# A hybrid decoder trunk: roots and decay exponents moved to GpSimd, the inverse's scratch moved to the residual's tiles, and a priority for each kind of mixer work

## The chip, the core and the metric

One core of a Trainium2 chip runs the whole program. The time is the device time of one execution in microseconds (us). The core's engines are named as in the profile: PE (TensorE, matrix multiplies; PEld is its weight load), DVE (VectorE), ACT (ScalarE), POOL (GpSimd) and SP (SyncE, which here issues most DMAs). PSUM is the memory that PE writes its results to; SBUF holds everything else on the core.

## The reference

Two layers over 256 tokens of 1,024 features in float32. Each layer is a half-step SwiGLU feed-forward, a token mixer, and another half-step feed-forward, each between two RMS norms:

```python
f = swiglu_ffn(rmsnorm(x, pre), w_in, w_out)          # D_FF = 2816
x = x + 0.5 * rmsnorm(f, post)
p = rmsnorm(x, pre) @ mix_w_in                        # q k v z beta a | glu | two gates
y = (sig(g_a) * gated_deltanet(...) + sig(g_b) * conformer_conv(...)) @ mix_w_out
x = x + rmsnorm(y, post)
...                                                   # the second feed-forward
```

The mixer's first branch is a gated delta rule with 8 heads of 128 and chunks of 64 tokens. q, k and v pass a causal convolution of 4 taps and SiLU; q and k are normalized per head and token. With G the running sum of the log decay in a chunk:

```python
decay = where(causal, exp(where(causal, G[c] - G[s], 0)), 0)
a_mat = where(strict, (k @ k.T) * decay * beta, 0)
u, w  = solve(I + a_mat, [v * beta, k * beta * exp(G)])
qk    = (q @ k.T) * decay
v_new = u - w @ state                                  # chunk after chunk
o     = (q * exp(G)) @ state + qk @ v_new
state = state * exp(G[-1]) + k_dec.T @ v_new
out   = (rmsnorm(o, norm_w) * silu(z)) @ w_o
```

The other branch is a gated linear unit, a causal depthwise convolution of 31 taps, a layer norm, SiLU and a projection.

## The kernel before, in words

**Weights.** All weight matrices stream in pieces of 128 x 1,024 numbers (some 128 x 544), 222 per layer, 90 of them in the mixer. SP loads a piece into `raw` (3 buffers), ACT rounds it to `whi`, and DVE or POOL subtracts to give the rest `wlo` (L147 and L148, rings of 8). PE multiplies in three products (`mm3`, L391 to L393; `piece_ch`, L416 to L418, gives results with channels on partitions): whi by the rounded activations, wlo by them, and whi by their rest. The set `POOL` lists which of a mixer's 90 pieces have their `wlo` made on POOL; all others are DVE's.

**The mixer's order.** PE's order is written out by hand: PE runs in program order, and the program runs the projection's column chunks in the order of `PLAN` (g0, k1, g1, ka, kb, ...), where an entry's list names the jobs that start when its chunk ends. A job is a generator; `Lanes.tick`, called after every few matmuls of a chunk, lets each job take its next step once the number of ticks in `DELAY` has passed and the jobs in `AFTER` are done. A chunk also starts only when the jobs in `BEFORE` are finished. So the jobs' PE instructions stand between the chunks' matmuls. On DVE, ACT and POOL a scheduler orders the instructions by priority; `CFG` holds offsets for some kinds (`stat`, `conv`, `ev`, `post`, ...), and a block inside `prio(tc, key)` gets the offset of its key.

**The steps that matter here.** `decays` (L668 to L693) makes the running sums G with three small PE products, sends them through DRAM to have them along the free axis (`gx`), and makes 16 exponents min(gx - G, mask) on DVE (`dt`, L687), the mask being copied into the unused part of the sums' PSUM tile (L678); ACT then takes the exponential. `k_tokens` (`kt0`, `kt1`) transposes k (L700), sums squares per head, takes their inverse root with `rsqrt`, and scales. `similarities` (`sim0`, `sim1`) multiplies k by k (L744), times decay and beta, into `at` (L747). `inverse` (L771, L773) inverts 32 x 32 blocks in 62 DVE steps per layer on two scratch tiles, `ia` and `iu`; they are slots 16 and 17, which q's convolution output `qT` uses too, and `AFTER` has both `f_q0` and `f_q1` wait for `inv`. `merge` joins the blocks' inverses to those of 64 x 64 (L804 to L831). `q_tokens` (`qt0`, `qt1`) transposes q, and makes the products `qk` (L867, L870). `s0` and `s1` (L895 to L928) run the two chunk steps. `cn` is the layer norm of the other branch, `on0` and `on` the norm of o.

**Roots.** `rms_scale` (L265) takes an inverse root of one column with a power on POOL. All other inverse roots use `rsqrt`: a bit-shift seed and three Newton steps on DVE, 8 or 16 columns wide, in a PSUM tile as scratch (tag `tr`, three buffers, which the transposes, the similarities and the sums also use).

Of the kernel before, what the change touches and what calls it, by code (L numbers as in the profile page):

```python
# [15 lines left out]
P = 128  # L16
# [50 lines left out]
POOL = {2, 3, 5, 9, *range(15, 54), *range(55, 65), 67, 68, 88}  # L67

CFG = dict(stat=0, conv=-800, ev=300, tok=4, st=4, post=50, pre=100, fin=None, tokens=0)


class Lanes:


    def __init__(self):
        self.now, self.jobs, self.done = 0, [], set()
# [37 lines left out]
def prio(tc, key):  # L114
    return nullcontext() if CFG[key] is None else tc.high_priority(offset=CFG[key])


class Stream:
# [14 lines left out]
    def load_one(self, parts=1):  # L133
        nc, src = self.nc, self.pieces[self.nload]
        n = src.shape[-1]
        raw = self.pool.tile([P, D], F32, name="raw", tag="raw", bufs=3)
        hi = self.pool.tile([P, D], F32R, name="whi", tag="whi", bufs=RING)
        lo = self.pool.tile([P, D], F32R, name="wlo", tag="wlo", bufs=RING)
        nc.sync.dma_start(raw[:, :n], src)
        eng = nc.gpsimd if self.side[self.nload] else nc.vector  # L140
        self.loaded.append((hi, lo))
        self.nload += 1
        for i in range(parts):
            if i:
                yield
            c = slice(i * n // parts, (i + 1) * n // parts)
            nc.scalar.copy(hi[:, c], raw[:, c])  # L147
            eng.tensor_tensor(lo[:, c], raw[:, c], hi.bitcast(F32)[:, c], op=ALU.subtract)  # L148
# [11 lines left out]
def trunk(ctx: ExitStack, tc: tile.TileContext, x_in, wfirst, consts, feat, pch, tokp,  # L160
# [29 lines left out]
    def ps_gd(shape=None):  # L190
        return psum.tile(shape or [P, 4, P], F32, name="gd", tag="tr", bufs=3)
# [3 lines left out]
    V, S, T = nc.vector, nc.scalar, nc.tensor  # L195
# [15 lines left out]
    mhalf = cpool.tile([P, 1], F32, name="mhalf")  # L211
    V.memset(mhalf, -0.5)
# [11 lines left out]
    negmask = cst[:, K_MASK:K_MASK + P]  # L224
# [15 lines left out]
    def rsqrt(o, v, n, scratch=None):  # L240

        y = work.tile([P, n], F32, name="nw_y", tag=f"nw_y{n}", bufs=2)
        seed = y if scratch is None else scratch[:, n:2 * n]
        V.tensor_scalar(seed.bitcast(I32), v.bitcast(I32), 1, None, op0=ALU.logical_shift_right)
        V.tensor_scalar(y.bitcast(I32), seed.bitcast(I32), -1, 0x5F3759DF, op0=ALU.mult, op1=ALU.add)
        if n == 1:
            hv = work.tile([P, n], F32, name="nw_h", tag=f"nw_h{n}", bufs=2)
            a = work.tile([P, n], F32, name="nw_a", tag=f"nw_a{n}", bufs=2)
            V.tensor_scalar(hv, v, -0.5, None, op0=ALU.mult)
            for it in range(3):  # L250
                V.tensor_scalar(a, y, y, hv, op0=ALU.mult, op1=ALU.mult)
                V.tensor_scalar(o if it == 2 else y, a, 1.5, y, op0=ALU.add, op1=ALU.mult)
            return
        hv, a = scratch[:, 0:n], scratch[:, n:2 * n]
        V.tensor_scalar(hv, v, -0.5, None, op0=ALU.mult)
        for it in range(3):
            V.tensor_tensor(a, y, hv, op=ALU.mult)
            V.tensor_tensor(a, y, a, op=ALU.mult)
            V.scalar_tensor_tensor(o if it == 2 else y, a, 1.5, y, op0=ALU.add, op1=ALU.mult)

    def rms_scale(o, ms, more=None):

        V.tensor_scalar(ms, ms, RMS_EPS if more is None else more, None if more is None else RMS_EPS,  # L263
                        op0=ALU.add, **({} if more is None else dict(op1=ALU.add)))
        nc.gpsimd.tensor_tensor(o, ms, mhalf, op=ALU.pow)  # L265
# [6 lines left out]
    lanes = Lanes()  # L272
# [259 lines left out]
    def mixer(xt, l, after_mix):  # L532
# [88 lines left out]
        rq = small(16, "rq", bufs=1)  # L621
        ex = small(32, "ex", bufs=1)
# [6 lines left out]
        def decays():  # L629
# [44 lines left out]
            V.tensor_tensor(xin[:, 16:32], xin[:, 16:32], ps[:, 0:16], op=ALU.subtract)  # L674
            gr = stt("gr", [P, P])[0:16]
            S.copy(gr, ps[0:16, 128:256])
            mask = ps[:, 256:384]
            S.copy(mask, negmask)  # L678
            gd = dram.tile([16, P], F32, name=f"gd{l}")
            nc.sync.dma_start(gd, gr)  # L680
            for gp in range(2):
                gx = slot(6 + gp, [P, 8, P], name="gx")
                row = gd[gp * 8:gp * 8 + 8, :].rearrange("a b -> (a b)").rearrange("(o n) -> o n", o=1)
                nc.sync.dma_start(gx.rearrange("p a b -> p (a b)"), row.broadcast_to([P, D]))
                dt = slot(8 + gp, [P, 8, P], name="dt")
                for th in range(8):
                    V.scalar_tensor_tensor(dt[:, th, :], gx[:, th, :], G[:, gp * 8 + th:gp * 8 + th + 1], mask,  # L687
                                           op0=ALU.subtract, op1=ALU.min)
                S.activation(dt, dt, AF.Exp)
                if gp == 0:  # L690
                    S.activation(ex, xin, AF.Exp)
# [14 lines left out]
        def k_tokens(gp):  # L706
# [18 lines left out]
            V.tensor_tensor(kds[:, c], ex[:, 16 + gp * 8:24 + gp * 8], t8, op=ALU.mult)
# [8 lines left out]
        def similarity(gp):  # L734
# [140 lines left out]
        def q_scale():  # L875
            yield from ()
            rsqrt(rq, vq, 16, ps_gd([P, 512]))
# [144 lines left out]
        def conv_norm():  # L1022
            xh = []
            for tb in range(2):
# [15 lines left out]
                rsqrt(r, ve, 1)  # L1040
# [27 lines left out]
        def o_scale(tb):  # L1068
# [5 lines left out]
            rqt = rq.rearrange("p (g b h) -> p g b h", g=2, b=2)[:, :, tb, :]  # L1074
            v8 = small(8, "vo")
            ve = v8.rearrange("p (g h) -> p g h", g=2)
            pw = ps_gd([P, 512])
            sq8 = pw[:, 16:24].rearrange("p (g h) -> p g h", g=2)
            V.tensor_copy(sq8, rqt)
            V.tensor_tensor(sq8, rqt, sq8, op=ALU.mult)  # L1080
            V.tensor_tensor(ve, sso, sq8, op=ALU.mult)
            V.tensor_scalar(v8, v8, 1.0 / P, RMS_EPS, op0=ALU.mult, op1=ALU.add)
            r8 = small(8, "ro")
            ry = pw[:, 24:32]
            rsqrt(ry, v8, 8, pw[:, 0:16])
            ro = r8.rearrange("p (g h) -> p g h", g=2)
            V.tensor_tensor(ro, rqt, ry.rearrange("p (g h) -> p g h", g=2), op=ALU.mult)
# [180 lines left out]
```

## Time and profile before

| | |
|---|---|
| runs | 1409.2, 1406.61, 1408.67 us; median 1408.67 |
| profiled execution | 1408.11 us, of which the span is 1406.0 |
| busy | PE 1362.3 us (97%), DVE 945.5, ACT 748.8, POOL 294.5 |
| mean granted PE clock | 0.988 |
| stages (us from the span's start) | feed-forward to 188, mixer to 503, feed-forward to 690 and 880, mixer to 1198, feed-forward to 1399 |

In a row of a timeline stand the start, the duration, the engine, the line, the operation, its tiles and shapes, and in brackets how long the engine idled before it and what released it. In a row of windows stand the window, its length, the busy time (and number of instructions) of PE, PEld, DVE, ACT and POOL, the granted clock, the DMA share and GB/s. A row of waits has the total idle time, how often, and the longest. In a row of groups stand the busy time and the mean in ns, and after the second bar the idle time ahead.

### The profile page before, as it was taken

What the parts mean: (1) busy time and instruction counts of PE and PEld (TensorE: products, weight loads), DVE (VectorE), ACT (ScalarE), POOL (GpSimd) and SP (SyncE); (2) the same over time, 40 slices, a digit from 0 to 9 for tenths busy, and PEclk for the clock granted to TensorE, in tenths of its full rate; (3) what the DMA queues carried; (4) which work ended last, traced back from release to release, by engine and by line L of the source; (5) the groups of instructions that cost most, each with busy time, mean ns of one, the idle gap of its engine ahead of it and who ended that gap; (6) DMA issues with size and microseconds to landing.
All of it is one profiled execution on the core that took longest, in us unless ns stands there. A gap on an engine that the chain in (4) does not pass through costs nothing.

```text
span 1406.0 us, 20213 instructions
## 1 busy us (share of the span) xinstructions
PE 1362.3 (97%) x7428; PEld 1157.0 (82%) x7428; DVE 945.5 (67%) x1876; ACT 748.8 (53%) x1182; POOL 294.5 (21%) x152
## 2 busy tenths in 40 slices
PE   8999999989999999999999999998999999999998
PEld 6888879888888888888878888797978888788886
DVE  5665457897969776554476553689978797765543
ACT  6554446856555556444355443666565664554441
POOL 0000035676630010000000000375755300100000
PEclk9999999999999999999999999998999999999999
DMA  7776655555443656555477655565544436575551
GB/s 260 231 210 182 193 168 181 194 145 171 143 150 105 217 200 225 187 180 184 144 226 213 190 176 171 173 202 167 161 148 135 150 119 211 165 238 186 188 181 59
DMA packets 82963, 250.67 MB, mean 178 GB/s; under 512 B 21136, under 2 KB 21680, under 8 KB 82864
## 3 DMA queue, kind: packets, MB, share of 16 engines
q1 hardware_dynamic: 82576, 249.32, 55.1%
q8 instruction: 58, 0.95, 0.3%
q14 instruction: 41, 0.34, 0.1%
q10 hardware_dynamic: 288, 0.07, 0.0%
HBM read 245.14 MB, written 4.21 MB: 177 GB/s over the span
## 4 chain that ended last, share of the span: by engine, by line
PE 84%; DVE 8%; DMA 3%; ACT 2%; issue 2%; POOL 1%; DVEq 0%; POOLq 0%; ACTq 0%; SPq 0%
PE mm L391 22%; PE mm L393 22%; PE mm L392 22%; PE mm L416 3%; PE mm L417 3%; PE mm L418 3%; DVE wlo L148 2%; PE tr L512 1%; DMA raw<-w2i 1%; DMA raw<-mw 1%; DVE cacc L595 1%; DVE dt L687 1%; DMA gx<-gd 1%; DVE iup L773 1%; DVE iu L771 1%
## 5 line engine op out<-in xcount | busy, mean ns | idle before, releaser
L147 ACT CAST whi<-raw 128x1024 fp32r<-128x1024 f32 (+2 forms) x445 | 463.3, 1042 | 438.5 <-PE mm L393 266.4
L148 DVE TENSOR_TENSOR wlo<-raw,whi 128x1024 fp32r<-128x1024 f32 (+1 forms) x333 | 407.7, 1228 | 290.8 <-ACT whi L147 285.8
L391 PE MATMUL mm<-whi,xt 128*128 128x512 f32 (+1 forms) x1024 | 410.0, 400 | 0.9 <-ACT whi L147 0.9
L392 PE MATMUL mm<-wlo,xt 128*128 128x512 f32 (+1 forms) x1024 | 398.8, 389 | 3.1 <-DVE ss L263 2.6
L393 PE MATMUL mm<-whi,xt 128*128 128x512 f32 (+1 forms) x1024 | 399.4, 390 | 0.4 <-DVE xt L270 0.4
L148 POOL TENSOR_TENSOR wlo<-raw,whi 128x1024 fp32r<-128x1024 f32 (+1 forms) x112 | 266.7, 2393 | 323.7 <-ACT whi L147 303.8
L393 PEld LDWEIGHTS mm<-whi,xt 128*128 128x128 f32 x1024 | 193.5, 189 | 41.8 <-DVE xt L270 1.1
L392 PEld LDWEIGHTS mm<-wlo,xt 128*128 128x128 f32 x1024 | 194.2, 190 | 40.4 <-DVE wlo L148 5.0
L391 PEld LDWEIGHTS mm<-whi,xt 128*128 128x128 f32 x1024 | 194.3, 190 | 37.5 <-ACT whi L147 1.3
L595 DVE SCALAR_TENSOR_TENSOR cacc<-hT,pc,cacc 128x254 f32<-128x254 f32 (+28 forms) x464 | 188.7, 463 | 21.2 <-ACT cacc L591 21.2
L416 PE MATMUL mm<-xt,whi 128*128 128x256 f32 x480 | 139.8, 291 | 1.6 <-ACT sg L578 1.6
L391 PE MATMUL mm<-whi,act 128*128 128x512 f32 x352 | 138.0, 392 | 0.0
L417 PE MATMUL mm<-xt,whi 128*128 128x256 f32 x480 | 137.4, 286 | 0.0
L418 PE MATMUL mm<-xt,wlo 128*128 128x256 f32 x480 | 137.3, 286 | 0.0
L393 PE MATMUL mm<-whi,act 128*128 128x512 f32 x352 | 137.2, 390 | 0.0
L392 PE MATMUL mm<-wlo,act 128*128 128x512 f32 x352 | 137.0, 389 | 0.0
L416 PEld LDWEIGHTS mm<-xt,whi 128*128 128x128 f32 x480 | 93.9, 196 | 2.1 <-ACT sg L578 2.0
L417 PEld LDWEIGHTS mm<-xt,whi 128*128 128x128 f32 x480 | 93.8, 195 | 0.1
L418 PEld LDWEIGHTS mm<-xt,wlo 128*128 128x128 f32 x480 | 93.7, 195 | 0.0
L265 POOL TENSOR_TENSOR rpost<-ss,mhalf 128x1 f32<-128x1 f32 x12 | 9.3, 774 | 393.3 <-DVE ss L263 393.3
L393 PEld LDWEIGHTS mm<-whi,act 128*128 128x128 f32 x352 | 66.1, 188 | 14.0
L391 PEld LDWEIGHTS mm<-whi,act 128*128 128x128 f32 x352 | 66.1, 188 | 13.5
(238 smaller groups left out, 1416.2 us busy)
## 6 DMA issues: line engine op xcount, KB each, us to landing
raw<-mw SPq DMA_DIRECT2D x168, 512.0 KB, 3.3
raw<-w1i SPq DMA_DIRECT2D x88, 512.0 KB, 4.3
raw<-w2i SPq DMA_DIRECT2D x88, 512.0 KB, 3.7
raw<-w1o SPq DMA_DIRECT2D x44, 512.0 KB, 3.6
raw<-w2o SPq DMA_DIRECT2D x44, 512.0 KB, 3.3
wbc<-feat SPq DMA_DIRECT2D x13, 512.0 KB, 5.4
raw<-mkb SPq DMA_DIRECT2D x8, 272.0 KB, 3.0
xs<-x SPq DMA_DIRECT2D x4, 512.0 KB, 3.5
```

Source lines behind the costliest of these rows:

```text
L147: nc.scalar.copy(hi[:, c], raw[:, c])
L148: eng.tensor_tensor(lo[:, c], raw[:, c], hi.bitcast(F32)[:, c], op=ALU.subtract)
L391: T.matmul(o, xh, wh, start=start, stop=False)
L392: T.matmul(o, xh, wl, start=False, stop=False)
L393: T.matmul(o, xl, wh, start=False, stop=stop)
L416: T.matmul(o, wh, xh, start=kt == 0 and b % 2 == 0, stop=False)
L417: T.matmul(o, wh, xl, start=False, stop=False)
L418: T.matmul(o, wl, xh, start=False, stop=kt == 7 and b % 2 == 1)
L512: T.transpose(tr[:, k, tb, :], a[:, 1, k * P:(k + 1) * P], ident)
L595: cur = V.scalar_tensor_tensor(accs[i][:, sh:], h_of(t)[:, :SEQ - sh], dw(t, KW - 1 - sh), accs[i][:, sh:], op0=ALU.mult, op1=ALU.add)
L687: V.scalar_tensor_tensor(dt[:, th, :], gx[:, th, :], G[:, gp * 8 + th:gp * 8 + th + 1], mask, op0=ALU.subtract, op1=ALU.min)
L771: V.tensor_tensor(tmp, u[:, 0:n, s:s + 1].broadcast_to([P, n, m]), a[:, s:s + 1, s + 1:32].broadcast_to([P, n, m]), op=ALU.mult)
```

## The change

- `rsqrt` is gone. `power` raises to -0.5, 0.5 or -1 with one POOL instruction (L250 after the change). The k scales, q scales, o scales and the layer norm use it, with the small products around it on POOL as well, in SBUF: no PSUM tile is used for a root.
- The exponents are 16 POOL instructions per layer (clamped to at most 0), without the mask; the decay tiles `DT` are masked later, after their use in `at`, by one POOL `affine_select` for each of the two halves.
- The inverse's `ia` and `iu` take the tags x0 and x1 (the residual's tiles, which lie in DRAM during the mixer, and later hold o). `f_q0` and `f_q1` no longer wait for `inv`.
- z0 (with s1, s0) and z1 (with merge) change places in `PLAN`; many `DELAY` numbers differ.
- `POOL` has 61 pieces per layer for 56.
- Each kind of job has a priority offset of its own (`KIND`, `CFG`), and so have the pieces' ACT and `wlo` instructions.

```diff
-POOL = {2, 3, 5, 9, *range(15, 54), *range(55, 65), 67, 68, 88}
-CFG = dict(stat=0, conv=-800, ev=300, tok=4, st=4, post=50, pre=100, fin=None, tokens=0)
+POOL = {3, 5, 12, *range(15, 69), 73, 82, 86, 88}
+CFG = dict(stat=-800, conv=-200, ev=-200, ..., tokens=100, glu=200, dec=200, kt=0, vt=0, qt=-800, inv=-200, sim=0, merge=0, scan=0, norm=0, onorm=0, yt=50, w=500)
...
     def step(self, job):
         try:
-            next(job[3])
+            with prio(self.tc, KIND.get(job[1])):
+                next(job[3])
...
+    def power(o, v, e):
+        nc.gpsimd.tensor_tensor(o, v, exps[e].broadcast_to(list(v.shape)), op=ALU.pow)
...
-            mask = ps[:, 256:384]
-            S.copy(mask, negmask)
...
-                    V.scalar_tensor_tensor(dt[:, th, :], gx[:, th, :], G[:, ...], mask,
-                                           op0=ALU.subtract, op1=ALU.min)
+                    W.tensor_scalar(dt[:, th, :], gx[:, th, :], G[:, ...], 0.0,
+                                    op0=ALU.subtract, op1=ALU.min)
...
-            ve, rk = small(8, "ve"), small(8, "rk")
-            ps = ps_gd([P, 512])
...
-            rsqrt(rk, ve, 8, ps[:, 8:24])
...
+            W.tensor_scalar(ve, ss, 1e-6, None, op0=ALU.add)
+            power(rk2, ve, -1.0)
+            W.tensor_tensor(sc[:, c], beta[:, c], rk2, op=ALU.mult)
+            W.tensor_tensor(kds[:, c], sc[:, c], ex[:, 16 + gp * 8:24 + gp * 8], op=ALU.mult)
+            power(irk[:, c], ve, 0.5)
...
+            W.affine_select(DT[gp], DT[gp], [[0, 8], [1, P]], ALU.is_ge, 0.0, 0, -1)
...
-            ia = slot(16, [P, D], name="ia")
-            buf = slot(17, [P, D], name="iu")
+            ia = slots.tile([P, D], F32, name="ia", tag="x0")
+            buf = slots.tile([P, D], F32, name="iu", tag="x1")
...
-            rsqrt(rq, vq, 16, ps_gd([P, 512]))
+            power(rq, vq, -0.5)
+            power(rq2, vq, -1.0)
...
-                rsqrt(r, ve, 1)
+                power(r, ve, -0.5)
...
-            rsqrt(ry, v8, 8, pw[:, 0:16])
...
+            W.tensor_tensor(ve, rq2t, sso, op=ALU.mult)
+            W.tensor_scalar(v8, v8, 1.0 / P, RMS_EPS, op0=ALU.mult, op1=ALU.add)
+            power(r8, v8, -0.5)
+            W.tensor_tensor(ro, ro, rqt, op=ALU.mult)
```

The order on POOL before, in layer 0's mixer, around the k scales (`kt` by `kds`); in these rows a name with a number is one buffer, and x18 means that many alike in a row:

```order
L148 TENSOR_TENSOR wlo<-raw,whi 128x1024
L148 TENSOR_TENSOR wlo<-raw,whi 128x544
L148 TENSOR_TENSOR wlo<-raw,whi 128x1024 x18
L727 TENSOR_TENSOR kt_1654<-kt_1654,kds 128x512
L148 TENSOR_TENSOR wlo<-raw,whi 128x1024
L727 TENSOR_TENSOR kt_1655<-kt_1655,kds 128x512
L148 TENSOR_TENSOR wlo<-raw,whi 128x1024 x23
```

The same place after; `dt` is an exponent or, in the last row, the masking, `rk` and `irk` are powers:

```order
L156 TENSOR_TENSOR wlo<-raw,whi 128x1024
L677 TENSOR_SCALAR dt<-gx,G 128x128 x8
L706 TENSOR_SCALAR ve<-ssk 128x8
L250 TENSOR_TENSOR rk_2668<-ve,exp_82 128x8
L250 TENSOR_TENSOR irk<-ve,exp_81 128x8
L708 TENSOR_TENSOR sc<-beta,rk_2668 128x8
L709 TENSOR_TENSOR kds<-sc,ex 128x8
L712 TENSOR_TENSOR kt_1658<-kt_1658,kds 128x512
L677 TENSOR_SCALAR dt<-gx,G 128x128 x6
L156 TENSOR_TENSOR wlo<-raw,whi 128x1024
L677 TENSOR_SCALAR dt<-gx,G 128x128 x2
L737 AFFINE_SELECT dt<-dt 128x1024
```

Where one product stood between two pieces, eight exponents, the k scales with two powers, a product and six more exponents stand there now, and a masking follows.

The order on DVE before, at the end of layer 0's inverse (`iu`, `iup`). q0's convolution has been summed by then, but its results, which ACT writes into `qT`, wait; `c_3607` is the first tile of q1's (L611):

```order
L771 TENSOR_TENSOR iu<-iup,ia 128x30
L773 TENSOR_TENSOR iup<-iup,iu 128x15x2
L771 TENSOR_TENSOR iu<-iup,ia 128x16
L773 TENSOR_TENSOR iup<-iup,iu 128x16
L611 SCALAR_TENSOR_TENSOR c_3607<-mm,pc,c_3607 128x255
L595 SCALAR_TENSOR_TENSOR cacc<-hT_1650,pc,cacc 128x254
L611 SCALAR_TENSOR_TENSOR c_3607<-mm,pc,c_3607 128x254
L703 TENSOR_REDUCE ssk<-sq 128x4
L611 SCALAR_TENSOR_TENSOR c_3607<-mm,pc,c_3607 128x253
```

The order on DVE after, where the inverse still has over 30 of its 62 steps ahead of it (the convolution is L602, the inverse L757 and L759, and `c_3581` q1's first tile):

```order
L757 TENSOR_TENSOR iu<-iup,ia 128x136
L602 SCALAR_TENSOR_TENSOR c_3581<-mm,pc,c_3581 128x255
L759 TENSOR_TENSOR iup<-iup,iu 128x8x17
L602 SCALAR_TENSOR_TENSOR c_3581<-mm,pc,c_3581 128x254
L757 TENSOR_TENSOR iu<-iup,ia 128x128
L602 SCALAR_TENSOR_TENSOR c_3581<-mm,pc,c_3581 128x253
L759 TENSOR_TENSOR iup<-iup,iu 128x8x16
L757 TENSOR_TENSOR iu<-iup,ia 128x135
L602 SCALAR_TENSOR_TENSOR c_3587<-mm,pc,c_3587 128x255
L759 TENSOR_TENSOR iup<-iup,iu 128x9x15
L602 SCALAR_TENSOR_TENSOR c_3587<-mm,pc,c_3587 128x254
```

q1's convolution moved from behind the inverse to between its steps, and the results of both can be written there.

The order on PE before, from the merge's last product (L831, of the second half) to the scan's first (L895); here each buffer has its number, `whi_3876` being one weight piece:

```order
L831 MATMUL gd_4104<-u_2642,at_2641 64x64 x8
L391 MATMUL mm_4072<-whi_3850,xt_1500 128x512
L392 MATMUL mm_4072<-wlo_3851,xt_1500 128x512
L393 MATMUL mm_4072<-whi_3850,xt_1500 128x512
L391 MATMUL mm_4071<-whi_3876,xt_1500 128x512
L392 MATMUL mm_4071<-wlo_3877,xt_1500 128x512
L393 MATMUL mm_4071<-whi_3876,xt_1500 128x512
L391 MATMUL mm_4071<-whi_3876,xt_1500 128x512
L392 MATMUL mm_4071<-wlo_3877,xt_1500 128x512
L393 MATMUL mm_4071<-whi_3876,xt_1500 128x512
L895 MATMUL gd_4174<-vr_3528,u_2642 128x128 x4
L895 MATMUL gd_4181<-vr_3338,u_2765 128x128 x4
```

The same on PE after (L811 and L817 are the merge's last steps, for both halves, L882 the scan's first):

```order
L811 MATMUL gd_4107<-at_2817 64x64 x8
L811 MATMUL gd_4117<-at_2689 64x64 x8
L817 MATMUL gd_4107<-u_2818,at_2817 64x64 x8
L817 MATMUL gd_4117<-u_2690,at_2689 64x64 x8
L382 MATMUL mm_4148<-whi_3843,xt_1503 128x512
L383 MATMUL mm_4148<-wlo_3844,xt_1503 128x512
L384 MATMUL mm_4148<-whi_3843,xt_1503 128x512
L882 MATMUL gd_4156<-vr_3505,u_2690 128x128 x4
L882 MATMUL gd_4163<-vr_3384,u_2818 128x128 x4
```

Where nine matmuls stood between the merge's last product and the scan's first, three stand now, and none stands between the merge's last two steps.

More of the change, by code (lines that the diff above doesn't have):

```diff
@@ L114, in prio @@
 def prio(tc, key):
-    return nullcontext() if CFG[key] is None else tc.high_priority(offset=CFG[key])
+    return nullcontext() if key is None or not CFG[key] else tc.high_priority(offset=CFG[key])
 class Stream:
@@ L146, in load_one @@
             c = slice(i * n // parts, (i + 1) * n // parts)
-            nc.scalar.copy(hi[:, c], raw[:, c])
-            eng.tensor_tensor(lo[:, c], raw[:, c], hi.bitcast(F32)[:, c], op=ALU.subtract)
+            with prio(self.tc, "w"):
+                nc.scalar.copy(hi[:, c], raw[:, c])
+                eng.tensor_tensor(lo[:, c], raw[:, c], hi.bitcast(F32)[:, c], op=ALU.subtract)
     def peek(self, i):
@@ L193, in trunk @@
     ctx.enter_context(tc.manual_schedule(engines={mybir.EngineType.PE}))
-    V, S, T = nc.vector, nc.scalar, nc.tensor
+    V, S, T, W = nc.vector, nc.scalar, nc.tensor, nc.gpsimd
     def xtile(tb):
@@ L210, in trunk @@
     V.memset(ones, 1.0)
-    mhalf = cpool.tile([P, 1], F32, name="mhalf")
-    V.memset(mhalf, -0.5)
+    exps = {e: cpool.tile([P, 1], F32, name=f"exp{i}") for i, e in enumerate((-0.5, 0.5, -1.0))}
+    for e, t in exps.items():
+        V.memset(t, e)
     warm = cpool.tile([P, 1], F32, name="warm")
@@ L239, in trunk @@
         pieces += [w2i[l, i] for i in range(44)] + [w2o[l, i] for i in range(22)]
[L240 to L259, printed above, removed]
+    def power(o, v, e):
+        nc.gpsimd.tensor_tensor(o, v, exps[e].broadcast_to(list(v.shape)), op=ALU.pow)
     def rms_scale(o, ms, more=None):
@@ L264, in rms_scale @@
                         op0=ALU.add, **({} if more is None else dict(op1=ALU.add)))
-        nc.gpsimd.tensor_tensor(o, ms, mhalf, op=ALU.pow)
+        power(o, ms, -0.5)
     def split(hi, lo, src):
@@ L621, in mixer @@
         rq = small(16, "rq", bufs=1)
+        rq2 = small(16, "rq2", bufs=1)
         ex = small(32, "ex", bufs=1)
```

41 lines of the change are left out of this document (15 added, 26 removed), and 21 rows, old and new, of tables (AFTER, DELAY, PLAN).

## The prediction

> **What bounds the kernel now.** I read the page's busy rows first, then the windows by stage, then PE's waits, then the timeline of the two stretches where they fall.
>
> ```profile
> PE 1362.3 (97%) x7428; PEld 1157.0 (82%) x7428; DVE 945.5 (67%) x1876; ACT 748.8 (53%) x1182; POOL 294.5 (21%) x152
> ...
> 188.00:503.00 315.00, 300.99 (x2005) 265.45 (x2004) 256.86 (x692) 189.99 (x353) 139.24 (x65) 0.98 0.52 168
> 503.00:690.00 187.00, 186.63 (x851) 153.94 (x850) 107.21 (x119) 90.38 (x113) 4.02 (x4) 1.00 0.58 192
> ...
> 880.00:1198.00 318.00, 303.52 (x1999) 267.63 (x1998) 257.17 (x691) 185.98 (x345) 139.39 (x66) 0.97 0.51 165
> ```
>
> PE is the bound and a feed-forward stage (the middle window) has nothing to give. The two mixers (188 to 503, 880 to 1198) hold 14.0 and 14.5 us of PE idle, and a granted clock of 0.98 and 0.97, which over 315 and 318 us is some 6 and 10 us more. Only these 44 us can be won. PE's waits say where they lie:
>
> ```profile
> PE gd L744 <- ACT kt L713: 7.8, 4, 2.8
> PE tr L700 <- ACT qT L613: 6.0, 4, 2.6
> PE tr L313 <- DVE xw L305: 4.4, 2, 2.2
> ...
> PE tr L700 <- ACT kt L713: 3.6, 2, 1.8
> PE gd L744 <- DVE at L747: 3.5, 2, 2.0
> ```
>
> The sums are over both layers. Three rows (7.8 + 3.6 + 3.5 = 14.9 us) are the stretch with decays, k tokens and similarities; one (6.0) is the start of the q tokens; one (4.4) is the mixer's entry. After such idling the clock falls too:
>
> ```profile
> 260.00:280.00 20.00, 16.55 (x126) 15.91 (x125) 16.43 (x49) 15.42 (x31) 9.51 (x4) 0.91 0.57 186
> 280.00:300.00 20.00, 15.16 (x126) 14.71 (x125) 19.90 (x87) 8.35 (x14) 11.46 (x6) 1.00 0.34 102
> 340.00:360.00 20.00, 17.84 (x84) 14.61 (x85) 13.90 (x37) 11.93 (x25) 8.23 (x4) 0.83 0.49 133
> 960.00:980.00 20.00, 14.83 (x102) 13.86 (x101) 16.85 (x61) 16.03 (x33) 7.67 (x4) 0.83 0.43 135
> 980.00:1000.00 20.00, 18.50 (x136) 18.21 (x135) 19.85 (x76) 6.24 (x7) 12.40 (x7) 0.83 0.51 147
> ```
>
> **The change: q tokens, a gain.** Before, q's convolution outputs sit in the inverse's two scratch tiles, so q's results wait for the end of the inverse. In DVE's, ACT's and PE's timeline and a window:
>
> ```profile
> 340.98 0.18 DVE L773 TENSOR_TENSOR iup<-iup,iu 128x16 f32<-128x16 f32 x1
> 341.04 0.42 ACT L613 ACTIVATE qT<-c 128x256 f32<-128x256 f32 x1 [2.33 <-DVE iu L771]
> 341.51 0.46 PE L700 MATMUL tr<-cst,qT 128*128 128x128 f32 x1 [2.58 <-ACT qT L613]
> 344.00:348.00 4.00, 4.00 (x12) 3.16 (x12) 2.24 (x5) 2.49 (x6) 1.54 (x1) 0.50 0.35 59
> ```
>
> The inverse's scratch moves to x's tiles, so q's results are written between the inverse's steps, long before the transposes that read them. What goes per layer: 3.0 us of idle (6.0 / 2), and the slow clock, 0.17 x 20 = 3.4 us in 340 to 360. I take 6.5 us per layer, 13 in all (bounds 6, the idle alone, to 15).
>
> Here a page speaks differently from the row. The Trainium skill ("TensorE: Matmul & The Clock Gate", Part 1) has the clock drop after a whole idle window of about 3.4 us. No single idle here reaches that (2.58), and yet 344 to 348 ran at 0.50, so the trace does not bear it out as a threshold for one gap. By the rule alone these stalls would cost their idle only, and the time would be 7 us later than my sum.
>
> **Decays, k tokens and similarities, a gain.** The mask is a copy in the decays' second PSUM tile, which therefore stays taken until the last of 16 exponents has run; the k scales keep a PSUM tile for their Newton steps too. Transposes (L700) and similarities (L744) rotate through what is left, behind ACT's queue:
>
> ```profile
> 268.18 0.24 ACT L678 COPY gd<-cst 128x128 f32<-128x128 f32 x1
> 268.54 1.28 ACT L691 ACT_TABLE_LOAD   x1
> 269.96 0.57 ACT L713 COPY kt<-tr 128x512 f32<-128x512 f32 x1
> 271.49 1.06 ACT L147 CAST whi<-raw 128x1024 fp32r<-128x1024 f32 x1
> 273.39 0.88 ACT L578 ACTIVATE sg<-mm,bgh 128x256 f32<-128x256 f32 x2
> ...
> 275.02 4.22 DVE L687 SCALAR_TENSOR_TENSOR dt<-gx,G,gd 128x128 f32<-128x128 f32 x16 [1.24 <-DMA gx<-gd]
> ...
> 285.84 0.28 PE L416 MATMUL mm<-xt,whi 128*128 128x256 f32 x1
> 285.96 0.28 PE L417 MATMUL mm<-xt,whi 128*128 128x256 f32 x1
> ```
>
> After, neither holds a tile: the decays' tile is free after ACT's small copies. Of the loss, idle is 14.9 / 2 = 7.5 us per layer; the clock adds 0.09 x 20 = 1.8 in layer 0 and 2 x 0.17 x 20 = 6.8 in layer 1, some of it while PE is idle anyway; I take 10. What is late next: the table load stays, and ACT's copy of the third transposes stands behind it. From the decay sums ACT has two small copies (0.5), the load (1.28), exponentials (0.5), a cast (1.06), gate activations (two 0.44 and two alike, 1.7), a square and the copy (2 x 0.57): 6.2, with gaps some 6.7. PE is there after twelve transposes (0.2 each) and twelve 256-column matmuls at 0.12, some 4.2. So about 2.5 us of idle stay, with 1 of clock. Gain 6.5 per layer, 13 in all (bounds 4 to 16). The later similarities hang on GpSimd: gx lands 8.8 us after the sums (275.02 - 268.18, and 2 before the mask copy), then come 8 exponents (2.8), scales (2.8) and four products (1.1), 15.5 in all, by the prices of the next part. PE, counted at 0.12 and 0.23 us a matmul, comes at 16.7 and with its idle at 19: 3.5 us to spare.
>
> **GpSimd, no cost while it keeps up.** It gets 5 more weight pieces per layer (61 for 56), the 16 exponents, two masks, ten powers and small products. The pieces are what PE multiplies by. Prices:
>
> ```profile
> L148 POOL TENSOR_TENSOR wlo<-raw,whi 128x1024 fp32r<-128x1024 f32 x110 | 264.0, 2412 | 304.7 <-ACT whi L147 303.8 <-PE mm L417 0.4
> L727 POOL TENSOR_TENSOR kt<-kt,kds 128x512 f32<-128x512 f32 x4 | 4.2, 1042 | 3.6 <-DVE kds L725 3.5
> L737 POOL MEMSET u<- 128x1024 f32 x4 | 3.8, 957 | 330.7 <-ACT jk L382 327.7 <-DVE x L388 3.0
> L148 POOL TENSOR_TENSOR wlo<-raw,whi 128x544 fp32r<-128x544 f32 x2 | 2.7, 1372 | 19.0 <-DVE cacc L595 19.0
> L808 POOL MEMSET at<- 32x256 f32 x4 | 1.2, 302 | 1.3 <-PE gd L804 1.3
> L265 POOL TENSOR_TENSOR rstd<-ss,mhalf x12: 549/554/1462, 18.6 to 1227.1; 128x1 f32<-128x1 f32 x12
> ...
> L148 DVE TENSOR_TENSOR wlo<-raw,whi 128x1024 fp32r<-128x1024 f32 x325 | 402.1, 1241 | 290.6 <-ACT whi L147 285.6
> ```
>
> An exponent (128x128, one tensor input) lies between the memset line, (957 - 302) / 768 = 0.85 ns a column, so 0.2 us, and the two-input line, 1372 / 544 x 128 = 0.32; I take 0.35 with its start, 5.6 us per layer (3 to 17, the end at 1.04 each being the 128x512 row). A mask on 128x1024 is between 0.96 (memset) and 2.41; I take 1.5, 3 us. A power of 8 columns is not in the trace: at least the 0.55 of one column, at most 8 x 0.55 = 4.4; of 16 columns 0.55 to 8.8. I take 1.2 and 2, nearer to the one-column row, since a piece 1,024 times wider costs but four times as much, so that most of such a 0.55 should be its start. From the first decay piece to the second mask GpSimd then has 5 pieces (12.1), 2 kt products (2.1), 5.6 + 3 + 4 powers (4.8) + small products (2.4) = 30 us of the 34 that PE takes there, where before it was busy 9.51 + 11.46 = 21 of 40. So nothing is added, with 4 to 5 us to spare. DVE in return loses Newton steps, exponents and pieces.
>
> **Merge and scan, given back.** PE's order in z0 and z1 is exchanged, the merge starts 48 matmuls later, and its steps stand closer: both L817 halves and the first scan product are 3 matmuls apart where they were 9, and so are the state product and the second u product. Before:
>
> ```profile
> 418.26 1.95 PE L912 MATMUL gd<-state,kT 128*128 128x128 f32 x16
> 419.35 2.16 DVE L915 SCALAR_TENSOR_TENSOR vr<-gd,neg_eg,vr 128x128 f32<-128x128 f32 x8 [0.90 <-PE gd L912]
> 422.55 0.39 PE L393 MATMUL mm<-whi,xt 128*128 128x512 f32 x1
> 422.78 1.95 PE L920 MATMUL gd<-vr,u 128*128 128x128 f32 x16
> L886 ACT COPY vn<-gd 128x512 f32<-128x512 f32 x4 | 2.4, 588 | 1.8 <-PE gd L920 1.3 <-PE gd L895 0.5
> ...
> L595 DVE SCALAR_TENSOR_TENSOR cacc<-hT,pc,cacc 128x254 f32<-128x254 f32 (+28 forms) x464 | 188.7, 463 | 21.2 <-ACT cacc L591 21.2
> ```
>
> vr ends at 421.51, 1.3 us ahead of the product that reads it (422.78); with six matmuls of 0.23 us fewer between, 1.4 us, this cover is just gone, and where DVE first ends a depthwise convolution (58 of the last row's steps, 188.7 / 8 = 24 us at most) it is overdrawn by about 1.3. The copies (0.59) between the other close steps give 0.4 to 0.6 at four places. Together 3.5 per layer, 4 with some slow clock: 8 in all (bounds 2 to 14). The bound below nothing is left out, since nothing stalls there now.
>
> **Entry and order.** The mixer's entry waits for xw:
>
> ```profile
> L305 DVE SCALAR_TENSOR_TENSOR xw<-x,rstd,wbc x8: 739/748/2836, 192.8 to 902.5; 128x512 f32<-128x512 f32 x8
> ```
>
> The slow ones (2836 for 748) run beside GpSimd's pieces, which remain. The new priorities put the statistics ahead elsewhere; I take 2 us of gain for all entries (0 to 4).
>
> **Sum.** The profiled execution took 1408.11 (span 1406.0), 0.6 under the median of the runs, so either serves: 1408.1 - 13 - 13 - 2 + 8 = 1388.
>
> **Rivals.** *GpSimd falls behind (slower).* For: it has 4 to 5 us to spare, and its queue is in order, so a late power holds every piece behind it. The point is a power of 8 columns at about 2.4 us. At 8/16 columns of 3.7/7 (0.45 a column), four cost 10 us more in the decays, 5 beyond the spare, the similarities stall 1.5 of it already, and two of 16 columns cost 10 more ahead of eight pieces, 5 past what they have; with the clock's fall after two such stalls (3.4 for one at the q tokens) some 14 us per layer, 1388 + 28 = 1416. Against: the row's mean of a piece suggests start-up rather than columns. I give 0.22. Beside it the Trainium skill ("GPSIMD Engine Reference", section 4.1) says that elementwise work belongs to VectorE, two-input work on GpSimd being about half as fast; the wlo rows agree (2412 to 1241). By that rule an exponent would be twice DVE's 340 ns, 5 us more per layer, about the spare: 1388 to 1392 and no other sign.
>
> *The gains come, but the compact merge eats more* (six of DVE's qk products now stand behind one such convolution, and PE reads none of them, but shares their PSUM tiles, at the merge's first product, which they reach with 2 us to spare): the 14 of the bound for 8, and 3 more per layer at that product, 1388 + 6 + 6 = 1400. Against: DVE has lost its Newton steps ahead of it. 0.17.
>
> *The change does not do what it says*: the third transposes still wait for ACT's table load, so the decays' idle stays, and only q gains, 13 + 2 - 8 = 7: 1401; with a large merge loss 1407, the same. 0.09, 0.06 of it the same.
>
> **Numbers.** Forecast 1388, 0.52, its own range 1376 to 1398. The two middle cases end at 1400 to 1407. With the slower case at 1412 to 1425, the range 1374 to 1414 leaves out 0.2. A difference under 0.2% (2.8 us) is about what a measurement of this kernel cannot tell from none. Faster 0.72, same 0.06, slower 0.22.
>
> **What would show it.** Right: in the new profile PE's wait for qT is gone and the clock at the q tokens 1.0; PE's waits in the decays sum to about 5 us over both layers rather than 15; new waits for vr, vn and u of 0.4 to 1.3 us. Wrong: PE waiting for wlo from GpSimd, a power of 8 columns above 2.4 us, or DVE's qk products late into the merge.

## The result, and the profile after

The changed kernel took 1409.29 us (median of 20 runs, 1405.02 to 1418.09), the kernel before 1409.22 (20 runs): a ratio of 1.0006, 95% interval 0.9993 to 1.002. The forecast was 1388. The time did not move, but nearly all of its parts did.

PE's waits after, from the changed kernel's profile (total us over both layers, times, longest). Its lines are numbered anew: L690 and L729 are the k transposes and the similarities, L732 `at`, L602 the four-tap convolution out of PSUM, L407 to L409 the products of `piece_ch`:

```profile
PE mm L407 <- DVE c L602: 15.6, 3, 7.5
PE gd L729 <- ACT kt L703: 5.5, 2, 2.8
PE gd L729 <- DVE at L732: 5.4, 2, 2.8
PE mm L407 <- ACT whi L155: 4.9, 1, 4.9
...
PE mm L382 <- ACT gate L957: 3.0, 4, 1.3
...
PE gd L782 <- DMA u<-dU: 0.7, 2, 0.4
...
PE tr L304 <- DVE xw L298: 0.3, 1, 0.3
```

The wait for qT (6.0) is gone, that for xw fell from 4.4 to 0.3, those for kt from 11.4 to 5.5; that for `at` rose from 3.5 to 5.4. In their place PE waits 15.6 us for the convolution to empty its PSUM tiles and 4.9 for a rounded weight piece. Both come behind the similarities. The windows there (PE, PEld, DVE, ACT, POOL busy, clock, DMA share, GB/s):

```profile
280.00:300.00 20.00, 17.36 (x136) 17.16 (x135) 5.56 (x17) 4.10 (x6) 19.42 (x24) 0.91 0.18 63
300.00:320.00 20.00, 9.98 (x76) 9.51 (x74) 13.75 (x38) 11.15 (x18) 18.33 (x13) 0.76 0.51 145
320.00:340.00 20.00, 18.13 (x130) 18.16 (x131) 15.04 (x47) 12.11 (x24) 13.86 (x7) 0.81 0.51 162
340.00:360.00 20.00, 20.00 (x129) 17.94 (x128) 16.70 (x57) 14.75 (x32) 15.67 (x7) 1.00 0.50 165
980.00:1000.00 20.00, 17.25 (x122) 17.05 (x121) 7.00 (x20) 8.67 (x12) 19.50 (x22) 0.83 0.16 39
1000.00:1020.00 20.00, 11.37 (x75) 10.93 (x74) 17.55 (x49) 9.54 (x16) 18.62 (x12) 0.76 0.60 187
```

From 280 to 300 GpSimd is full (19.42 of 20), while DVE does 5.56 us and ACT 4.10; PE still has matmuls to run (17.36). From 300 to 320 PE pays: 9.98 us of work, at a clock of 0.76, and in the 20 us behind that the clock is still 0.81. The q tokens' window (340 to 360) is full at clock 1.00, as forecast. GpSimd's timeline in that stretch:

```profile
279.95 5.56 POOL L677 TENSOR_SCALAR dt<-gx,G 128x128 f32<-128x128 f32 x8 [3.19 <-DMA gx<-gd]
285.60 0.25 POOL L706 TENSOR_SCALAR ve<-ssk 128x8 f32<-128x8 f32 x1
285.94 1.68 POOL L250 TENSOR_TENSOR rk<-ve,exp 128x8 f32<-128x8 f32 x1
287.59 1.65 POOL L250 TENSOR_TENSOR irk<-ve,exp 128x8 f32<-128x8 f32 x1
289.20 0.20 POOL L708 TENSOR_TENSOR sc<-beta,rk 128x8 f32<-128x8 f32 x1
...
290.78 4.17 POOL L677 TENSOR_SCALAR dt<-gx,G 128x128 f32<-128x128 f32 x6
294.92 2.39 POOL L156 TENSOR_TENSOR wlo<-raw,whi 128x1024 fp32r<-128x1024 f32 x1
297.28 1.41 POOL L677 TENSOR_SCALAR dt<-gx,G 128x128 f32<-128x128 f32 x2
298.64 1.10 POOL L737 TENSOR_SCALAR_AFFINE_SELECT dt<-dt 128x1024 f32<-128x1024 f32 x1
300.80 2.42 POOL L156 TENSOR_TENSOR wlo<-raw,whi 128x1024 fp32r<-128x1024 f32 x1 [1.05 <-ACT whi L155]
...
305.28 1.64 POOL L250 TENSOR_TENSOR irk<-ve,exp 128x8 f32<-128x8 f32 x1
306.88 0.20 POOL L708 TENSOR_TENSOR sc<-beta,rk 128x8 f32<-128x8 f32 x1
```

From the first exponent (279.95) to the end of the second `sc` (307.08) GpSimd needs 27.1 us in layer 0 (26.0 in layer 1), with one pause of 1.05 us. Two engines stand behind that series with their queues in order. A row each of ACT's and of DVE's waits:

```profile
ACT dt L679 <- POOL dt L677: 31.4, 4, 10.4
DVE at L732 <- POOL sc L708: 27.9, 4, 10.1
```

And the timelines of ACT, DVE and PE at that place:

```profile
298.72 1.06 ACT L679 ACTIVATE dt<-dt 128x1024 f32<-128x1024 f32 x1 [10.35 <-POOL dt L677]
299.69 1.03 ACT L155 CAST whi<-raw 128x1024 fp32r<-128x1024 f32 x1
...
301.15 0.58 ACT L692 ACTIVATE sq<-tr 128x512 f32<-128x512 f32 x1
...
301.76 0.69 DVE L693 TENSOR_REDUCE ssk<-sq 128x4 f32<-128x512 f32 x1 [6.76 <-ACT sq L692]
...
307.12 1.12 DVE L732 SCALAR_TENSOR_TENSOR at<-gd,sc,dt 128x128 f32<-128x128 f32 x4 [3.92 <-POOL sc L708]
...
309.28 0.47 DVE L602 SCALAR_TENSOR_TENSOR c<-mm,pc,c 128x255 f32<-128x255 f32 x1
...
315.83 0.55 PE L407 MATMUL mm<-xt,whi 128*128 128x256 f32 x1 [7.47 <-DVE c L602]
```

ACT waits for the second half's exponents (10.35 us), with the weight casts behind them, and behind those k's squares (`sq`). DVE waits 6.76 us for these squares: the sum that the second half's `sc` needs hangs on the exponents too. Then DVE waits for `sc`, with `c` behind its products: `c` empties the PSUM tiles that PE needs, so PE stands still from 308.4 to 315.83.

### The profile page after: what moved, and what is told of

The parts are those of the page before. It is cut to its first block, busy times and chain, and to the rows that moved or that the text cites. A ratio compares the mean times of both kernels' runs of the same rounds, so it can differ in the third digit from the quotient of the medians.

```text
span 1407.2 us, 20073 instructions
## 1 busy us (share of the span) xinstructions
PE 1358.6 (97%) x7428; PEld 1157.3 (82%) x7428; DVE 898.4 (64%) x1630; ACT 750.9 (53%) x1180; POOL 374.5 (27%) x244
## 4 chain that ended last, share of the span: by engine, by line
PE 81%; POOL 6%; DVE 4%; DMA 4%; ACT 2%; issue 2%; SPq 0%; POOLq 0%; DVEq 0%; ACTq 0%
PE mm L384 22%; PE mm L382 22%; PE mm L383 22%; DMA raw<-mw 2%; POOL wlo L156 2%; PE mm L407 2%; PE mm L408 2%; PE mm L409 2%; POOL dt L677 2%; PE tr L503 1%; DVE cacc L586 1%; ACT whi L155 1%; DVE wlo L156 1%; DVE c L602 1%; DMA raw<-w2i 1%
## 5 line engine op out<-in xcount | busy, mean ns | idle before, releaser
L156 DVE TENSOR_TENSOR wlo<-raw,whi 128x1024 fp32r<-128x1024 f32 (+2 forms) x323 | 394.1, 1223 | 288.0 <-ACT whi L155 283.5
L156 POOL TENSOR_TENSOR wlo<-raw,whi 128x1024 fp32r<-128x1024 f32 (+1 forms) x122 | 287.9, 2370 | 214.4 <-ACT whi L155 205.3
L586 DVE SCALAR_TENSOR_TENSOR cacc<-hT,pc,cacc 128x254 f32<-128x254 f32 (+28 forms) x464 | 182.5, 463 | 12.7 <-ACT cacc L582 12.7
L407 PE MATMUL mm<-xt,whi 128*128 128x256 f32 x480 | 142.8, 298 | 20.7 <-DVE c L602 15.6
L408 PE MATMUL mm<-xt,whi 128*128 128x256 f32 x480 | 139.7, 291 | 0.0
L409 PE MATMUL mm<-xt,wlo 128*128 128x256 f32 x480 | 139.4, 291 | 0.0
L407 PEld LDWEIGHTS mm<-xt,whi 128*128 128x128 f32 x480 | 96.2, 200 | 21.9 <-issue 16.3
L250 POOL TENSOR_TENSOR rpost<-ss,exp 128x1 f32<-128x1 f32 x12 | 6.5, 542 | 390.9 <-DVE ss L254 390.9
L408 PEld LDWEIGHTS mm<-xt,whi 128*128 128x128 f32 x480 | 96.2, 200 | 0.1
L409 PEld LDWEIGHTS mm<-xt,wlo 128*128 128x128 f32 x480 | 95.9, 200 | 0.0
L722 POOL MEMSET u<- 128x1024 f32 x4 | 3.8, 956 | 332.8 <-ACT jk L373 327.5
L384 PEld LDWEIGHTS mm<-whi,act 128*128 128x128 f32 x352 | 66.1, 188 | 13.9
```

The costliest lines, as they stand in the source:

```text
L384: T.matmul(o, xl, wh, start=False, stop=stop)
L407: T.matmul(o, wh, xh, start=kt == 0 and b % 2 == 0, stop=False)
L408: T.matmul(o, wh, xl, start=False, stop=False)
L409: T.matmul(o, wl, xh, start=False, stop=kt == 7 and b % 2 == 1)
L586: cur = V.scalar_tensor_tensor(accs[i][:, sh:], h_of(t)[:, :SEQ - sh], dw(t, KW - 1 - sh), accs[i][:, sh:], op0=ALU.mult, op1=ALU.add)
```

## The experiments

The theory was that the forecast gains are there and that GpSimd's series gives them back.

**Undo one part: exponents on DVE.**

```diff
-                    W.tensor_scalar(dt[:, th, :], ...
+                    V.tensor_scalar(dt[:, th, :], ...
```

> The changed kernel with one word changed: the 16 exponents per layer run on DVE again (still clamped at 0 and masked later). Theory (GpSimd's queue is the loss): the exponents are 16 x 0.71 = 11.4 us of the 27 us per layer during which GpSimd works without a pause from gx's landing to the second half's sc, and DVE is idle for 14 us there. Without them sc comes some 9 to 11 us earlier, PE's waits for DVE's c and for whi (7.5 + 4.4 and 4.9 + 3.7 us) go with most of the slow clock behind them: 1385 to 1392 us. Rival A (the five more pieces make GpSimd late): GpSimd is still full behind the stretch, 1400 or more. Rival B (the closer order of steps costs it): 1405 or more.

Measured: 1413.5 us, ratio 1.0042 (1.0023 to 1.006). The waits for `c` shrank, but others came. PE's waits in it:

```profile
PE mm L407 <- DVE c L602: 10.3, 3, 4.4
...
PE gd L907 <- DVE vr L902: 5.3, 4, 2.5
...
PE gd L782 <- DMA u<-dU: 3.9, 1, 3.9
PE gd L729 <- DVE at L732: 3.8, 1, 3.8
PE gd L782 <- ACT whi L155: 3.7, 1, 3.7
PE gd L811 <- issue: 2.6, 2, 1.3
```

My theory missed here: merge and scan now wait 15.5 us (the rows of vr, u, L811 and L782's whi). DVE does convolution, inverse, convolution, then `vr`, each behind the other (the inverse's PSUM tile has the depthwise convolution's tag, `cacc`; here, in the kernel before and in the changed one it starts 0.2 to 0.5 us after that convolution's last step). The word changed also made the scheduler reorder DVE, and 25 us lay between the last `at` and the inverse where the changed kernel has 19. So this run undoes more than one thing and decides nothing about the series.

**One part alone: q without the inverse.** The kernel before, with

```diff
-    "vt1": ("f_v1", "kt1"), "f_q0": ("inv",), "f_q1": ("inv",),
+    "vt1": ("f_v1", "kt1"),
-            ia = slot(16, [P, D], name="ia")
-            buf = slot(17, [P, D], name="iu")
+            ia = slots.tile([P, D], F32, name="ia", tag="x0")
+            buf = slots.tile([P, D], F32, name="iu", tag="x1")
```

> The kernel before with one part of the change: the inverse's scratch in the residual's tiles, and q's chunks no longer waiting for the inverse. Theory (the q gain is real, and lost elsewhere in the change): PE's wait for qT (6.0 us over both layers) and the slow clock behind it go, 1394 to 1399 us. Rival (the gain is not real: the same time is waited for later, at the merge or the qk products): 1404 or more.

Measured: 1399.34 us, ratio 0.9945 (0.9924 to 0.9966). That is just above the theory's range and well below the rival's. The gain is real; the wait for qT is gone.

**The pieces as before.** The changed kernel with the old set `POOL`.

> The changed kernel with the weight pieces dealt out as before (56 per layer on GpSimd for 61). Theory (exponents and powers in series): the pieces inside the critical stretch are the same ones, so the waits of 7.5 and 4.4 us stay: 1405 to 1412 us. Rival A (five more pieces make GpSimd late): the waits shrink by some 12 us per layer, 1390 to 1396.

Measured: 1436.71 us, ratio 1.0215 (1.0194 to 1.0236). Neither theory expected this. PE's waits:

```profile
PE mm L407 <- DVE c L602: 22.3, 4, 6.5
PE gd L907 <- DVE vr L902: 13.5, 2, 6.8
...
PE tr L304 <- DVE xw L296: 4.4, 2, 2.2
```

The wait for xw is back at exactly the 4.4 of before, under the new priorities: it was the set of pieces that ended it. With five pieces more on DVE, in an order that the scheduler changed too, DVE is late for `vr` (13.5), and the waits for `c` grew (15.6 to 22.3). So taking the five pieces from GpSimd did not help; that they relieve DVE there is likely, but this run does not separate it from the new order.

**Shorten the series.** Two kernels that leave a part out, and both together:

```diff
-            power(rk2, ve, -1.0)
+            W.tensor_scalar(rk2, ve, 1e-6, None, op0=ALU.mult)
...
-            power(irk[:, c], ve, 0.5)
+            W.tensor_scalar(irk[:, c], ve, 0.01, None, op0=ALU.mult)
```

> The changed kernel with the two powers of 8 columns of each k scale replaced by a multiplication by a constant (leaves out the inverse root and the root of k's norms). Theory: four powers of 1.66 us become four of about 0.25, 5.6 us less in series per layer, so PE's waits in the stretch shrink by 5 to 8 us per layer with some clock: 1394 to 1400 us. Rival (the powers lie beside other waiting, the exponents alone decide): 1405 to 1410.

```diff
                 for th in range(8):
+                    if th:
+                        W.memset(dt[:, th, :], -1.0)
+                        continue
```

> The changed kernel with seven of each eight exponents replaced by a fill with -1 (leaves out most decay exponents); PE's order is the same and DVE's and ACT's nearly so. Theory (the series on GpSimd from gx's landing to the second sc is the loss): 14 x some 0.5 us leave the series per layer, 14 us in all; the powers' run turned 11.2 us off the series into 8.5 us of time, so 1396 to 1401 us. Rival (the exponents are not on the path, only the powers are): 1406 or more.

> The changed kernel with both: seven of eight exponents a fill, and the k scales' two powers a multiplication by a constant (leaves out both). Theory: the series on GpSimd is then about as short as the prediction took it to be, and the time is about what it forecast: 1386 to 1393 us, with PE's wait for DVE's c nearly gone. Rival (the other parts of the change lose by themselves, in merge and scan): 1398 or more even so.

**Shorten it and compute everything.** First one power for each scale and one subtraction for each half; then the clamp on ACT, as exp(-relu(-d)):

```diff
-            power(rk2, ve, -1.0)
+            power(rk2, ve, -0.5)
+            W.tensor_tensor(irk[:, c], ve, rk2, op=ALU.mult)
+            W.tensor_tensor(rk2, rk2, rk2, op=ALU.mult)
...
-            power(rq2, vq, -1.0)
+            W.tensor_tensor(rq2, rq, rq, op=ALU.mult)
...
-                for th in range(8):
-                    W.tensor_scalar(dt[:, th, :], gx[:, th, :], G[:, ...], 0.0, ...)
+                gb = G[:, ...].rearrange(...).broadcast_to([P, 8, P])
+                W.tensor_tensor(dt, gx, gb, op=ALU.subtract)
+                W.tensor_scalar(dt, dt, 0.0, None, op0=ALU.min)
```

> The changed kernel, whole in what it computes, with a cheaper series: one power to -0.5 for each scale (its square and its product with the sum give the other two), and the eight exponents of a half as one subtraction of 128x1024 with G broadcast and one clamp. Theory: 2.5 us of powers and some 2.2 x 2 us of exponents leave the series per layer (if the subtraction is as long as a weight piece, 2.4, and the clamp 1.1), 14 us in all: 1396 to 1402 us. Rival (a subtraction with a broadcast operand costs no less than the eight): 1404 or more.

```diff
-                W.tensor_scalar(dt, dt, 0.0, None, op0=ALU.min)
-                S.activation(dt, dt, AF.Exp)
+                S.activation(dt, dt, AF.Relu, scale=-1.0)
+                S.activation(dt, dt, AF.Exp, scale=-1.0)
```

> The seventh run's kernel with the clamp moved from GpSimd (2.78 us for 128x1024) to ACT, as a Relu of the negated difference ahead of the exponential; whole in what it computes, PE's order the same and DVE's and ACT's nearly so. Theory (length of the series on GpSimd): 2 x 2.8 us per layer leave it, 11 us in all, and ACT, idle for most of that stretch, gains 2 x 1.06: 1384 to 1390 us, faster than both kernels. Rival (ACT's queue takes the place of GpSimd's: the casts behind the two Relus come late): 1393 or more.

The series is taken as above, from the start of the first exponent to the end of the second `sc`, in each layer. PE's order is the same in all of these, DVE's and ACT's the same but for 14 rows at most:

| kernel | series, us, layer 0 and 1 | time, us | ratio to before (95%) |
|---|---|---|---|
| changed | 27.1, 26.0 | 1409.29 | 1.0006 (0.9993 to 1.002) |
| one power, one subtraction | 22.4, 22.4 | 1395.8 | 0.9903 (0.9872 to 0.9934) |
| k powers cheap | 21.7, 20.6 | 1400.77 | 0.9955 (0.9936 to 0.9974) |
| one power, one subtraction, clamp on ACT | 16.8, 16.8 | 1384.58 | 0.983 (0.9809 to 0.9851) |
| exponents cheap | 16.4, 16.4 | 1389.72 | 0.986 (0.9834 to 0.9886) |
| both cheap | 11.4, 11.6 | 1377.32 | 0.977 (0.9739 to 0.98) |

From first to last the series shrinks by 15.7 and 14.4 us, 30.1 in all, and the time by 32.0 (33 by the ratios, each of which is good to some 3 to 4 us): about one for one. The cleanest single step, the clamp moved to ACT, takes 11.2 us off the two series and 11.2 off the time (10 by the ratios). The powers' run lies just above its range: 8.5 us of time for 10.9 of series. I reckoned the next with that lower rate; the exponents' run and the run of both then came out 6 and 9 us below their ranges. With the series at 11.4, PE's wait for `c` is 1.9 us, and the mean granted clock 0.996 for 0.984. The clamp on ACT gives a kernel that computes everything and beats both, 1384.58 us. In this kernel and the one without that step the q scales lose a power too, which the series does not count. Two groups in the run with the clamp still on GpSimd say why it works:

```profile
L678 POOL TENSOR_SCALAR dt<-dt 128x1024 f32<-128x1024 f32 x4 | 11.1, 2776 | 0.2
L677 POOL TENSOR_TENSOR dt<-gx,G 128x1024 f32<-128x1024 f32 x4 | 7.6, 1897 | 3.8 <-DMA gx<-gd 3.8
```

The clamp (2776 ns) is dearer than the subtraction (1897), which comes to 0.24 us for each of eight heads.

**Before, with q and the entry.** The second run's kernel with

```diff
-POOL = {2, 3, 5, 9, *range(15, 54), *range(55, 65), 67, 68, 88}
+POOL = {3, 5, 12, *range(15, 54), *range(55, 65), 67, 68, 88}
```

> The kernel before with the q part (inverse's scratch in the residual's tiles) and, of the new set of pieces, only its first part: pieces 2 and 9 go to DVE and 12 to GpSimd. Theory (the mixer's entry gains because no piece runs on GpSimd beside xw): PE's wait for xw falls from 4.4 to below 1 us, 1394 to 1397 us. Rival (the entry gained by the new priorities): the wait stays at 4.4, 1398 to 1401 us.

Measured: 1394.2 us, ratio 0.9897 (0.9867 to 0.9928). The wait for xw fell to 1.5 us, not below 1; the entry's theory holds in its cause. In this run no xw runs beside a piece and none takes more than 753 ns; with the old set back (third run) one in each layer runs beside a piece again and takes 2834 and 2827 ns. What is left of the wait is no slow xw.

**Exponents on DVE, shorter powers.** The first run's kernel with one power for each scale.

> The first run's kernel (exponents on DVE) with one power for each scale. Theory (that run lost its gain because DVE's order came out another way, and merge and scan waited 15 us): those waits are there again in PE's rows, while the waits for c shrink by a few us: 1400 to 1410 us. Rival (it lost because the series was still too long, which 2.5 us less per layer mends): 1390 to 1398 us and no waits in the merge.

Measured: 1400.13 us, ratio 0.9952 (0.993 to 0.9975). The merge and scan still wait (vr 2.8, u 2.8, L811 2.6), at half the size, and `c` 8.5: the theory's side, at its edge.

**Let DVE work while it waits.** The changed kernel and the best one, with `sim=-300` for `sim=0`.

> The changed kernel with one number changed: the similarities' priority (sim) from 0 to -300, below the depthwise convolution's, so that DVE runs the convolution's remaining steps ahead of the products that wait for sc; GpSimd's series is as long as before. Theory (DVE stands idle behind those products, 27.9 us over both layers, and so v's convolution, the inverse and all that follows on DVE slide): DVE's idle for sc falls below 15 us and the inverse ends 8 us or more earlier after the sums than the 96.5 and 92.3 us of the changed kernel; PE then waits earlier, for the products' PSUM tiles, so the time falls only by part: 1398 to 1405 us. Rival (the length of the series sets the time through the products, whatever DVE does meanwhile): 1407 to 1415 us.

> The ninth run's kernel (one power, one subtraction, clamp on ACT) with the same number changed. Theory: with the short series DVE waits little in either order, and the products' PSUM tiles are held for the convolution's 16 us instead: no gain, 1383 to 1392 us. Rival (blocking on DVE still costs there, as PE's 10 us of waits for c show): 1376 to 1381 us.

Measured: 1479.87 and 1462.89 us (ratios 1.0512, 1.0484 to 1.0539, and 1.04, 1.0366 to 1.0434), 60 us and more above every range given. What was meant came: no wait of DVE for `sc` of any size is left, and in the first of the two the inverse ended 83.3 and 84.8 us after the sums (layer 0 and 1) for 96.5 and 92.3. But the scheduler then put a whole depthwise convolution (58 steps, 21.8 us) between the qk products, twice per layer; PE's row, in the second kernel alike one line further down:

```profile
PE gd L853 <- DVE qk L856: 70.7, 2, 35.3
```

Taking the 70.7 us off would leave 1409 and 1392, by this estimate no gain beside it. Whether an order exists that fills DVE's waiting without this is open.

## Why the prediction was wrong, point by point

- **GpSimd, no cost while it keeps up: the step that failed**, first by size. An exponent took 0.71 us where I took 0.35, a power of 8 columns 1.64 to 1.68 (1.2), one of 16 columns 2.90 (2), a mask 1.10 (1.5). All lay inside my bounds, but I added up values that were low where it mattered, twice over in series. My prices for that series are 5.6 (exponents) + 6.0 (two scales up to `sc`) + 4.8 (two pieces) + 1.0 (a product) + 1.5 (a mask), 18.9 us, against 27.1 and 26.0 measured. In layer 0 the exponents took 11.1 us for 5.6, the two scales 7.6 for 6.0, the mask 1.1 for 1.5, and 1.05 us was a wait for a cast that no term had. By the table's one for one the 8.2 and 7.1 us are about 15 of the 21 us between forecast and result; the other 6 are what the terms below come to together, and are not separated. The 0.35 came from the width of the operation, and left out that it is two operations, of which the clamp is the slow one. The Trainium skill ("GPSIMD Engine Reference", section 4.1) makes GpSimd about half as fast as VectorE for two-input work, and puts one-input work at roughly line rate. My sentence on that rule doubled DVE's 340 ns, the price of the old exponent, which read the mask as a second tensor; the new one has a single tensor input. On DVE that took 0.28 us (first experiment), so on GpSimd it was two and a half times as long: the line rate is not borne out here, and that the doubled 0.68 lies near 0.71 is luck.
- **Its mechanism failed too.** I looked for late pieces behind GpSimd and asked whether its busy time (30 us of 34) leaves room. That sum says nothing of when the second half's `sc` is done, and I gave no time for it. I did not name what stands behind the waiting instructions on DVE and ACT: `c` and the inverse behind `at`, the casts and k's squares behind the exponential. The slower rival had the cause, a late GpSimd, but looked for it in the powers: a power of 8 columns came out well below its 2.4 us, and the exponents were the larger excess. Nor did it have the road by which PE is reached.
- **q tokens: right, and oversized.** Forecast 13 us; alone it gave 0.55% of 1407.4, 8 us (5 to 11). The idle went (6.0), and the clock from 340 to 360 was 1.00 for 0.83. But from 260 to 300 it was 0.84 and 0.91 for 0.91 and 1.00, with the idle of the decays and similarities as before (15.0 us for 14.9). So in these two profiles a part of the slow clock moved instead of going; why is open.
- **Decays: the PSUM part right.** 2.5 us of idle behind the table load were to stay in each layer; 2.8 and 2.6 did. (Twelve transposes and twelve matmuls at my prices are 3.8 us, not the 4.2 that I wrote, which makes it 2.9.) The spare of 3.5 us before the later similarities was not there: PE waits 2.6 and 2.8 us for `at`, as the exponents and the first scale ahead of it took 9.5 us (279.95 to 289.40), where I had 5.6; that alone uses up the 3.5.
- **Merge and scan: oversized.** Forecast 8 us given back; the gate (3.0) and u (0.7) are what came, and with the clamp on ACT less than 1 us. The `vr` wait of 1.3 us is not in the changed kernel; it shows where DVE is later (5.3 and 13.5 above).
- **Entry: right in sign, undersized.** Forecast 2; xw's wait fell by 4.1, and the cause was the set of pieces. I had said that GpSimd's pieces remain beside xw; in the changed kernel none does, and the slowest xw takes 752 ns for 2836.
- **What would show it wrong** named a power above 2.4 us, PE waiting for GpSimd's `wlo`, or late qk products; none came, and the kernel was still 21 us late. Of the signs of being right, the idle for qT went, but the waits in the decays were 10.9 us rather than about 5. The two middle rivals looked elsewhere: the merge gave back less than forecast, not more, and the decays' wait for kt did fall (11.4 to 5.5).

## What to carry to other kernels

Moving work to an idle engine is priced by the longest series that it forms there ahead of someone who waits, not by that engine's share of busy time: GpSimd, 27% busy over the whole span, was full for 27 us. Follow each result of that series to the queue that waits for it, and read what is queued behind the waiting instruction. A fused operation that looks like one pass can hold one slow half; split it, and give that half to the engine that stands idle in the same stretch.

## What the runs showed of the hardware that I had not expected

- **Powers on GpSimd** cost 0.54 us for one column, 1.64 to 1.67 for eight and 2.90 for sixteen, which comes to about 0.16 us a column and 0.4 of start (an estimate from these three). Groups of the changed kernel (mean ns after the busy time):

```profile
L677 POOL TENSOR_SCALAR dt<-gx,G 128x128 f32<-128x128 f32 x32 | 22.2, 714 | 5.3 <-DMA gx<-gd 5.3
L250 POOL TENSOR_TENSOR rq<-vq,exp 128x16 f32<-128x16 f32 x4 | 11.5, 2896 | 1.0 <-DVE vq L845 1.0
L250 POOL TENSOR_TENSOR rk<-ve,exp 128x8 f32<-128x8 f32 x4 | 6.7, 1671 | 0.3
L250 POOL TENSOR_TENSOR rstd<-ss,exp 128x1 f32<-128x1 f32 x12 | 6.5, 542 | 53.8 <-DVE ss L254 53.8
L737 POOL TENSOR_SCALAR_AFFINE_SELECT dt<-dt 128x1024 f32<-128x1024 f32 x4 | 4.4, 1108 | 0.0
```

- **A piece on GpSimd can hold DVE until it ends.** With the exponents on DVE, one took 280 ns in the middle and 2383 at most (min, median and max of that line):

```profile
L677 DVE TENSOR_SCALAR dt<-gx,G x32: 273/280/2383, 279.3 to 983.8; 128x128 f32<-128x128 f32 x32
```

In its timeline, seven took 4.35 us. Two of them were held: one took 1.07 us, to the end of the `kt` product on GpSimd, and the next 2.38 us, to the end of the piece behind it. Powers did not do this: in layer 1, eight exponents took 1.66 us together beside two of them.

```profile
285.94 4.35 DVE L677 TENSOR_SCALAR dt<-gx,G 128x128 f32<-128x128 f32 x7
...
285.80 1.12 POOL L712 TENSOR_TENSOR kt<-kt,kds 128x512 f32<-128x512 f32 x1
286.88 2.34 POOL L156 TENSOR_TENSOR wlo<-raw,whi 128x1024 fp32r<-128x1024 f32 x1
...
982.40 1.66 DVE L677 TENSOR_SCALAR dt<-gx,G 128x128 f32<-128x128 f32 x8 [0.72 <-DMA gx<-gd]
...
981.33 1.79 POOL L250 TENSOR_TENSOR rk<-ve,exp 128x8 f32<-128x8 f32 x1
982.98 1.64 POOL L250 TENSOR_TENSOR irk<-ve,exp 128x8 f32<-128x8 f32 x1
```

The Trainium skill ("GPSIMD Engine Reference", section 1) has GpSimd share SBUF interfaces with DVE, with contention for DVE's two-port forms and for two SBUF inputs; these rows agree that the two contend, here for a DVE operation of one tensor input; whether that is a two-port form no row says, and beside the powers there was no contention.
